# Spreading the weighted bias of a routed expert FFN over every fourth expert step

## The chip, the core and the metric

The kernel runs on one core of one Trainium2 chip. The metric is the device time of one execution in microseconds (us); lower is better. TensorE (PE), VectorE (DVE), ScalarE (ACT) and GpSimd (POOL) each work through their own queue of instructions in order; SyncE (SP) issues most transfers, and POOL issues the gathers, the scatters and the accumulating transfers. TensorE's clock has two levels, 1.2 and 2.4 GHz, and the profile gives the granted clock as a share of the upper one.

## The reference: what is computed

One layer of an encoder over 1024 tokens of 1024 channels, float32. A mixing sub-layer (Fourier branch and attention) comes first, and then the part that matters here, a routed expert FFN: each token picks 4 of 32 experts.

```python
h = xb @ w_gate_up[e] + b_gate_up[e]
gate, up = h[:, :D_EXPERT], h[:, D_EXPERT:]
gate = jnp.minimum(gate, SWIGLU_LIMIT)
up = jnp.clip(up, -SWIGLU_LIMIT, SWIGLU_LIMIT)
act = (up + 1.0) * gate * jax.nn.sigmoid(SWIGLU_ALPHA * gate)
return act @ w_down[e] + b_down[e]
...
contrib = jnp.where(buf_valid[:, None], y.astype(jnp.float32) * buf_w[:, None], 0.0)
out = jnp.zeros((n, d), jnp.float32).at[buf_tok].add(contrib)
```

After it a residual and a layer norm give the output. Since b_down does not depend on the token, the sum over a token's experts of weight times b_down is one small matrix product: (tokens x 32 weights) by (32 x 1024 biases). The kernel computes it apart from the experts.

## The kernel before

All large products are done in a split form: a float32 weight is turned into a rounded part `whi` (ACT, line 147) and a remainder `wlo` (DVE, line 148), and both are multiplied.

**Expert steps.** Each expert has 8 chunks of the gate and up product (G1, 0 to 7), for the small ones two transpositions (TR, 12 and 13), and 4 chunks of the down product (G2, 8 to 11). Every G1 or G2 chunk reads 1 MB of weights through three buffers each of `wraw`, `whi` and `wlo`. Experts are ranked by load. Those with room for more than 128 tokens form lane A, the others lane B, and `moe_plan` merges the two lanes into one list of 420 (rank, chunk) pairs, the steps. It begins: steps 0 to 3, rank 31 chunks 0 to 3 (lane B, 64 tokens); steps 4 to 6, rank 9 chunks 0 to 2 (lane A, 192 tokens); 7 and 8, rank 31 chunks 4 and 5; 9 rank 9; 10 rank 31; 11 rank 9; 12 rank 31 chunk 7; 13 to 17, rank 9 chunks 5 to 7 with rank 31's transpositions between; 18, 19, 21, 22 are rank 31's down chunks, and its result is scattered after step 22; 20, 23, 26, 29 are rank 9's down chunks; 24, 25, 27, 28, 30, 31, 33, 35 are rank 30's G1 chunks (lane B); 32, 34, 36, 38, 40 are the first G1 chunks of rank 0 (lane A, 416 tokens), and step 37 and 39 are rank 30's transpositions.

**Lane B, `rows`.** Two chunks fill one PSUM tile `psr`, of which there is one. After the second of them (an odd chunk) ACT copies half of it into an SBUF tile `gur` (line 1177), DVE adds the other half (line 1178), and the activation follows in place. `psr` is free for the next two chunks after line 1178. There are two buffers of `gur`.

**The weighted bias, `bias_out(i)`**, for 128 tokens at a time, twice 512 channels. It takes one of two PSUM tiles `psd` (lane A's down product uses the same two) and one of the same two `gur` buffers, and it adds into the accumulator `acc_d` in DRAM by an accumulating transfer on POOL's queue:

```python
ab = pep.tile([P, 512], F32, name="psd")
pe_.matmul(ab, ct[:, i, :], bd[:, ns], start=True, stop=True)
t = pe.tile([P, 2, 256], F32, name="gur").rearrange("p a f -> p (a f)")
tail[0] = act.activation(t, ab, AF.Copy)
pool.dma_start(acc_d[i * P:(i + 1) * P, ns], t, accum_op=ALU.add)
```

**Scatters.** After an expert's last down chunk its rows are added into `acc_d` by an indirect accumulating transfer on POOL's queue (line 991). Gathers of the tokens of the next expert (line 987) go through the same queue; a gather needs the expert's table of slots, which SP loads (line 1072) when the expert before is at its chunk 1.

**`overflow()`** works out on DVE, from the counts of tokens, which blocks a loop after the experts must still do. It holds one `psd` tile from its first product to line 1291, and SP writes its two small results to DRAM (lines 1297 and 1298) in the queue that loads the weights.

**Order.** The list of steps is the order in which the instructions are written, but not exactly that in which an engine gets them: a list scheduler places each engine's instructions by its own model of time, and one that is ready can be placed ahead of earlier ones. A tool inserts the semaphores. The bias is written at steps 2 to 9, `overflow()` at step 12.

Of the kernel before, what the change touches and what calls it, by code (L numbers as in the profile page):

```python
# [26 lines left out]
NX = S // P  # L27
# [79 lines left out]
def layer_kernel(ctx, tc, x, c, w_ada, b_ada, w_in, q_norm_g, k_norm_g, w_fourier, w_attn_o, w_out,  # L107
# [922 lines left out]
    with tc.tile_pool(name="pew", bufs=3, side=RIGHT) as pew, tc.tile_pool(name="pes", bufs=1, side=RIGHT) as pes, \  # L1030
# [220 lines left out]
        def bias_out(i):  # L1251

            for n in range(2):
                ns = slice(n * 512, (n + 1) * 512)
# [5 lines that stand above are left out]
# [56 lines left out]
                    e.xt(b, h, ("ptr", "psr")[h])  # L1316
        for step, (r, i) in enumerate(plan):
            e, nx = ex_[r], follow.get(r)
            if step == 12:
                with tc.issue_after(tail[0].ins):  # L1320
                    overflow()
            if 2 <= step < 2 + NX:
                bias_out(step - 2)
            if i == 0:
                e.start()
            nb_ = len(nx.blocks) if nx else 0
            if i in G1:
                if i == 1 and nx:
                    nx.table()
                e.chunk(i)  # L1330
                if 2 <= i < nb_ + 2:
                    nx.fetch(i - 2)
            elif i in TR:
                e.at(i - TR[0])
            else:
                halves = [(b, h) for b in range(nb_) for h in range(2)][2 * (i - 8):2 * (i - 8) + 2]
                e.chunk(i, [partial(nx.xt, *bh) for bh in halves])
# [143 lines left out]
```

## Time and profile before

| | us |
|---|---|
| median of 3 runs (2807.48 to 2818.73) | 2810.29 |
| the profiled execution, its own time | 2809.73 |
| its span in the profile | 2808.0 |
| PE busy in the span (91%) | 2544.5 |
| DVE busy (74%) | 2083.0 |
| ACT busy (51%) | 1421.8 |

The experts take the span from about 1047 us to about 2760 us. In the rows below a wait is put down to the instruction that ended it; matmuls are pipelined, so the time of one of them overlaps with that of the next.

### The profile page before, as it was taken

Reading aid. Unit: us, or ns where it says so; the run is one execution under the profiler, and the core shown is the slowest. Engines: PE = TensorE matmul, PEld = TensorE weight load, DVE = VectorE, ACT = ScalarE, POOL = GpSimd, SP = SyncE. Lnnn points to the kernel's source line nnn. Section 1 sums busy time; section 2 is a strip of 40 time slices with the busy share of each in tenths; the row PEclk is TensorE's granted clock in tenths of the full one; section 3 lists DMA queues with packets and bytes.
Section 4 is the critical chain, followed back from the end, with each engine's and each line's share of the span. In section 5 each row is a group of like instructions: output and inputs, shape, how many; then the busy total and the mean of one; then the engine's idle time right before and its main releaser. Section 6 shows DMA issues by size and latency. Waiting matters only on the chain. (4 is left out here: it accounts for less than half of the span.)

```text
span 2808.0 us, 43022 instructions
## 1 busy us (share of the span) xinstructions
PE 2544.5 (91%) x15948; PEld 2307.1 (82%) x15948; DVE 2083.0 (74%) x3672; ACT 1421.8 (51%) x2190; POOL 380.1 (14%) x283
## 2 busy tenths in 40 slices
PE   6999999899999947889989989989999999998991
PEld 5888899799888946789889888977888888897881
DVE  7543438777755956868788888969896888887885
ACT  3411122466621535645566556647665665665562
POOL 3100012211032232000201010011101010020003
PEclk9999999999999958999999999999999999999996
DMA  6154411000054349857889799978988898988774
GB/s 229 55 185 158 160 55 31 16 1 1 1 179 145 121 150 259 250 173 251 255 273 290 239 292 282 301 230 276 287 282 247 273 295 272 290 285 257 248 250 152
DMA packets 468742, 561.23 MB, mean 200 GB/s; under 512 B 26632, under 2 KB 404944, under 8 KB 468480
## 3 DMA queue, kind: packets, MB, share of 16 engines
q1 hardware_dynamic: 448672, 494.41, 53.9%
q0 software_dynamic: 18768, 59.64, 8.4%
q10 hardware_dynamic: 1088, 4.39, 0.5%
q8 instruction: 127, 2.08, 0.3%
q14 instruction: 87, 0.71, 0.1%
HBM read 512.90 MB, written 46.82 MB: 199 GB/s over the span
## 5 line engine op out<-in xcount | busy, mean ns | idle before, releaser
L148 DVE TENSOR_TENSOR wlo<-wraw,whi 128x1024 fp32r<-128x1024 f32 x768 | 909.7, 1217 | 220.1 <-ACT whi L147 216.0
L147 ACT ACTIVATE whi<-wraw 128x1024 fp32r<-128x1024 f32 x768 | 767.9, 1051 | 462.8 <-DMA wraw<-in_w_gate_up_dram 130.7
L1128 PE MATMUL psg<-xTa,wlo 128*128 128x160 f32 (+7 forms) x1792 | 469.5, 278 | 3.1 <-DVE wlo L148 3.0
L1128 PEld LDWEIGHTS psg<-xTa,wlo 128*128 128x128 f32 x1792 | 341.6, 194 | 8.4 <-DVE wlo L148 6.1
L1124 PE MATMUL psg<-xTa,whi 128*128 128x320 f32 (+3 forms) x1024 | 307.1, 367 | 12.4 <-ACT whi L147 10.7
L141 PE MATMUL psd<-whi,aTa 128*128 128x256 f32 (+2 forms) x768 | 220.6, 291 | 27.1 <-ACT aTa L1152 17.6
L1126 PE MATMUL psg<-xTa,whi 128*128 128x256 f32 (+3 forms) x768 | 233.3, 308 | 11.3 <-ACT whi L147 9.1
L1127 PE MATMUL psg<-xTa,whi 128*128 128x256 f32 (+3 forms) x768 | 231.9, 305 | 0.0
L143 PE MATMUL psd<-whi,aTa 128*128 128x256 f32 (+2 forms) x768 | 216.8, 287 | 3.5 <-DVE aTa L1153 3.3
L142 PE MATMUL psd<-wlo,aTa 128*128 128x256 f32 (+2 forms) x768 | 217.5, 285 | 0.1
L1124 PEld LDWEIGHTS psg<-xTa,whi 128*128 128x128 f32 x1024 | 195.8, 194 | 23.5 <-ACT whi L147 13.2
L141 PEld LDWEIGHTS psd<-whi,aTa 128*128 128x128 f32 (+2 forms) x768 | 145.7, 190 | 36.1 <-ACT aTa L1152 21.2
L1126 PEld LDWEIGHTS psg<-xTa,whi 128*128 128x128 f32 x768 | 147.4, 192 | 14.9 <-ACT whi L147 10.8
L991 POOL DMA_INDIRECT acc_d<-xya,tab x33 | 60.6, 1836 | 654.0 <-DVE xya L1215 544.2
L143 PEld LDWEIGHTS psd<-whi,aTa 128*128 128x128 f32 (+2 forms) x768 | 145.0, 190 | 5.0 <-DVE aTa L1153 4.4
L1127 PEld LDWEIGHTS psg<-xTa,whi 128*128 128x128 f32 x768 | 147.5, 192 | 1.3
L1169 PE MATMUL psr<-wlo,xTb 128*128 128x512 f32 x352 | 145.1, 412 | 3.2 <-DVE wlo L148 3.1
L142 PEld LDWEIGHTS psd<-wlo,aTa 128*128 128x128 f32 (+2 forms) x768 | 145.9, 190 | 1.3 <-DVE wlo L148 0.4
L1168 PE MATMUL psr<-whi,xTb 128*128 128x512 f32 x352 | 144.6, 411 | 2.4 <-ACT whi L147 2.4
L147 ACT ACTIVATE wh<-wraw 128x1024 fp32r<-128x1024 f32 (+1 forms) x35 | 48.1, 1377 | 154.4 <-PE psg L206 92.9
L152 ACT ACTIVATE pth<-pst 128x512 fp32r<-128x512 f32 x128 | 75.1, 599 | 86.4 <-PE pst L632 85.1
L141 PE MATMUL pz<-wh,uh 128*128 128x256 f32 x384 | 110.4, 288 | 2.4 <-DVE mrow L480 2.4
(455 smaller groups left out, 6407.5 us busy)
## 6 DMA issues: line engine op xcount, KB each, us to landing
wraw<-in_w_gate_up_dram SPq DMA_DIRECT2D x512, 512.0 KB
wraw<-in_w_down_dram SPq DMA_DIRECT2D x128, 1024.0 KB
wa<-in_w_ada_dram SPq DMA_DIRECT2D x24, 1024.0 KB
wraw<-in_w_in_dram SPq DMA_DIRECT2D x13, 1024.0 KB
xs<-in_x_dram SPq DMA_DIRECT2D x8, 512.0 KB
m_d<-sgm POOLq DMA_DIRECT2D x8, 512.0 KB, 4.1
sa_d<-sgm POOLq DMA_DIRECT2D x8, 512.0 KB, 2.9
wraw<-in_w_attn_o_dram SPq DMA_DIRECT2D x8, 512.0 KB
```

Of the source, the lines that this page charges most:

```text
L141: pe_.matmul(o, lh, rh, start=start, stop=False)
L142: pe_.matmul(o, lh, rl, start=False, stop=False)
L143: pe_.matmul(o, ll, rh, start=False, stop=stop)
L147: act.activation(hi, raw, AF.Copy)
L148: (lo_eng or vec).tensor_tensor(lo, raw, f32(hi), op=ALU.subtract)
L152: act.activation(hi, ps, AF.Copy)
L1124: pe_.matmul(ps[:, :2 * n], wh[:, k, cs], xT[:, 4 * h + k, :, :], start=first, stop=False)
L1126: pe_.matmul(ps[:, :n], wh[:, k, cs], xh, start=first, stop=False)
L1127: pe_.matmul(ps[:, :n], wh[:, k, cs], xl, start=False, stop=False)
L1128: pe_.matmul(ps[:, :n], wl[:, k, cs], xh, start=False, stop=last)
L1168: pe_.matmul(o, xk, wh[:, k, :], start=False, stop=False)
L1169: pe_.matmul(o, xk, wl[:, k, :], start=False, stop=last)
```

## The change

Two constants of the loop over the steps. `bias_out(0)` to `bias_out(7)` are written ahead of steps 8, 12, 16, 20, 24, 28, 32 and 36 in place of steps 2 to 9, and `overflow()` ahead of step 40 in place of step 12. No operation is added or removed.

```diff
         for step, (r, i) in enumerate(plan):
             e, nx = ex_[r], follow.get(r)
-            if step == 12:
+            if step == 40:
                 with tc.issue_after(tail[0].ins):
                     overflow()
-            if 2 <= step < 2 + NX:
-                bias_out(step - 2)
+            if 8 <= step < 8 + 4 * NX and step % 4 == 0:
+                bias_out(step // 4 - 2)
             if i == 0:
                 e.start()
```

## Rows read from the trace of the kernel before

**Rows 1.** Stretches: us, busy us (instructions) of PE, PEld, DVE, ACT, POOL; PEclk, DMA share, GB/s
```profile
1047.00:1135.00 88.00, 68.98 (x349) 59.89 (x349) 54.30 (x99) 51.73 (x87) 20.08 (x20) 0.86 0.82 229
1135.00:1207.00 72.00, 55.57 (x298) 47.59 (x298) 62.47 (x121) 46.02 (x66) 9.46 (x6) 0.88 0.90 280
...
1207.00:1250.00 43.00, 42.44 (x221) 41.47 (x222) 23.60 (x39) 14.37 (x26) 0.00 (x0) 0.96 0.38 127
```

**Rows 2.** Waits of PE, 1054 to 1135 us: us in total, times, longest
```profile
PE psd L1256 <- ACT gur L1258: 8.0, 3, 4.6
PE psr L1164 <- DVE gur L1178: 3.7, 1, 3.7
PE psg L1124 <- ACT whi L147: 2.6, 3, 1.0
```

**Rows 3.** Waits of PE, 1135 to 1208 us
```profile
PE psr L1164 <- DVE gur L1178: 7.5, 2, 4.7
...
PE psd L1203 <- DVE xya L1215: 1.8, 1, 1.8
PE psd L141 <- ACT aTa L1152: 1.7, 1, 1.7
PE psr L1203 <- DVE gur L1178: 1.5, 1, 1.5
```

**Rows 4.** Waits of ACT, 1054 to 1135 us
```profile
ACT gur L1258 <- DMA acc_d<-gur: 15.1, 9, 4.5
ACT gur L1177 <- DMA acc_d<-gur: 4.6, 2, 2.5
```

**Rows 5.** ACT in order of time: start, us, operation, idle before and releaser
```profile
1055.14 0.59 ACT L1177 ACTIVATE gur<-psr 64x512 f32<-64x512 f32 x1
1055.76 0.60 ACT L1258 ACTIVATE gur<-psd 128x512 f32<-128x512 f32 x1
...
1077.66 0.60 ACT L1258 ACTIVATE gur<-psd 128x512 f32<-128x512 f32 x1 [4.53 <-DMA acc_d<-gur]
...
1080.77 0.59 ACT L1177 ACTIVATE gur<-psr 64x512 f32<-64x512 f32 x1
...
1085.36 0.60 ACT L1258 ACTIVATE gur<-psd 128x512 f32<-128x512 f32 x1 [1.40 <-DMA acc_d<-gur]
...
1118.42 0.60 ACT L1258 ACTIVATE gur<-psd 128x512 f32<-128x512 f32 x1 [2.50 <-DMA acc_d<-gur]
...
1122.44 0.59 ACT L1177 ACTIVATE gur<-psr 64x512 f32<-64x512 f32 x1 [2.45 <-DMA acc_d<-gur]
...
1133.78 0.59 ACT L1177 ACTIVATE gur<-psr 64x512 f32<-64x512 f32 x1 [2.18 <-DMA acc_d<-gur]
...
1169.76 0.59 ACT L1177 ACTIVATE gur<-psr 64x512 f32<-64x512 f32 x1
```

**Rows 6.** POOL in order of time
```profile
1131.90 0.86 POOL L1259 DMA_DIRECT2D acc_d<-gur  x1 [3.41 <-ACT gur L1258]
1165.52 1.05 POOL L987 DMA_INDIRECT xyb<-u_d,tab  x1 [32.75 <-PE psr L1169]
1166.87 1.49 POOL L991 DMA_INDIRECT acc_d<-xyb,tab  x1 [0.31 <-issue]
...
1356.89 1.56 POOL L991 DMA_INDIRECT acc_d<-xya,tab  x1 [6.26 <-DMA acc_d<-xya,tab]
```

**Rows 7.** Transfers, 1054 to 1250 us: a queue's packets, MB, share; an issue's count, size, landing
```profile
q0 software_dynamic: 3616, 8.91, 20.2%
...
acc_d<-gur POOLq DMA_DIRECT2D x16, 256.0 KB, 7.3
```

**Rows 8.** SP in order of time
```profile
1155.80 0.42 SPq L1072 DMA_DIRECT2D tab<-slot_d  x1
```

**Rows 9.** PE in order of time
```profile
1028.70 1.22 PE L1256 MATMUL psd<-bd,ct 128*128 128x512 f32 x2 [0.69 <-ACT ct L929]
```

## The prediction

> **What bounds the kernel now.** I read the stretches first, to see where TensorE is not the bound. From 1207 us, when the first large expert begins, it is busy 42.44 of 43 us, and the transfer engines work at a share of 0.38. Ahead of that lie the steps that the change touches: 1047 to 1135 us (rank 31's G1 and rank 9's G1), where PE is busy 68.98 of 88 us at a granted clock of 0.86, and 1135 to 1207 us (the down chunks of both, and rank 30's G1), 55.57 of 72 us at 0.88 [rows 1]. So 19 and 16 us of PE are idle there, and some of the busy time runs at the lower of the two clock levels. No later stretch is changed by the diff.
>
> Next, what ends those waits. In the first stretch the largest is 8.0 us in which PE has the next product of the bias to do and both `psd` tiles are still waiting for ACT's copy into `gur`; then 3.7 us for `psr`, and 2.6 us for a rounded weight [rows 2]. The cause is one engine on: ACT stands 15.1 us in nine places at the copy of line 1258 and 4.6 us in two at line 1177, each time until an accumulating transfer out of `gur` has landed [rows 4]. Everything else of ACT, the rounding of weights too, is queued behind it.
>
> The order of ACT's instructions then shows who holds whom. `gur` goes round in the order in which its users are written. Between lane B's copies at 1080.77 and 1122.44 us stand ten copies of the bias, the first at 1085.36 and the last at 1118.42 [rows 5]; in the code these ten are `bias_out(2)` to `(6)`, written between chunks 3 and 5 of rank 31. One buffer is taken for 0.86 us of issue and 7.3 us to landing [rows 6, 7], so two buffers pass one copy per 4.1 us, and ten need 41 us: lane B's copies are 41.7 us apart. The bias, not the experts, paces this stretch, and lane B's weights occupy their buffers meanwhile.
>
> **The change, part by part.**
>
> *The early crowd goes.* Ahead of rank 31's chunk 5 now stand two copies instead of ten, and ahead of chunk 7 two as before; six (steps 16, 20, 24) come before rank 30's first copy. Of the waits this takes: 8.0 for `psd`, 3.7 for `psr`, and the 1.5 that rank 31's down product waits after the copy of 1133.78 us [rows 2, 3, 5], together 13.2. Pairs still go through two buffers, and six copies between the copies of steps 12 and 25 want 25 us, so I take 11; the ends are 8 (only the product's own wait) and 13.2. The late rounding, 2.6 [rows 2], goes in part: 1.5, ends 0 and 2.6. Clock: 68.98 us of work at 0.86 would take 9.7 us less at the full level [rows 1]; part of that comes from the idle time ahead of the first step and stays, so I take 4, ends 0 and 9.7. Together 16.5 us, ends 8 and 25.5.
>
> A cap on it: the transfer engines are busy 0.82 of 88 us and 0.90 of 72 us, 137 of 160 us [rows 1]; 23 us at most can be squeezed out before they are the bound. The bias' own traffic is 16 x 256 KB, 4.2 of the 8.91 MB on POOL's queue, and by bytes 18.6 of the 39.6 us (20.2% of 196) that this queue takes of all 16 engines [rows 7]. Only the pairs of steps 32 and 36, a quarter or 4.7 us, leave for the stretch with a share of 0.38. So the cap is above what I take, but not far.
>
> *`overflow()` goes to step 40.* It holds one of two `psd` tiles while rank 9's first down chunk needs them: 1.8 us of PE waiting for line 1215. Its short operations stand on DVE where DVE is busy 62.47 of 72 us; 1.7 us of PE wait there for a split that DVE and ACT deliver late [rows 1, 3]. I take 2.5, ends 0 and 3.5. At step 40 what hides it is rank 0's G1, where DVE is busy 23.60 of 43 us and no down chunk wants `psd`. Without that cover the same 3.5 us would come back. Its two small writes on SP move along; weights queued behind them are covered by the slow chunks of rank 0.
>
> *A new wait at step 24.* This is the price. Before, all bias transfers were issued by 1131.90 us and the first scatter came at 1166.87 [rows 6]; none had to wait for a scatter. Now the pair of step 24 is written behind rank 31's scatter (after step 22). Both add into `acc_d`, and where one scatter follows another the second waits: 6.26 us behind the end of the first [rows 6]. The scatter itself stood behind the gather of 1165.52 us, which needs the table that SP issued at 1155.80 [rows 6, 8]. With those times: scatter issued until 1168.36, landed 1174.6, the first transfer of the pair issued until 1175.5, landed 1182.8. Its `gur` buffer is what rank 30's first copy needs, which ran at 1169.76 [rows 5]. So that copy comes 13.0 us later, and behind it on ACT stand the rounded weights and on PE the next `psr` chunks, whose wait there is already the longest, 4.7 us [rows 3]. One down chunk of rank 9 can be done meanwhile, no more, since the next one wants `psd` behind the bias of step 28. I take 9 of the 13; the ends are 0 (the pair gets ahead, or the gather and scatter come earlier with the shorter stretch) and 13.
>
> What the Trainium skill would make of this wait: DMA: Bandwidth & Descriptors, section Anatomy of one DMA, gives a transfer on POOL's path about 2.0 us plus its bytes over 436 GB/s, so 2.6 us for 256 KB. By it, as an estimate, the buffer would be back at 1174.4 and the copy only 4.7 us late, about one chunk's cover, and the sum below would be 2792. The measured 7.3 us [rows 7] speaks against it.
>
> *The pairs of steps 28, 32 and 36.* Step 28's is followed at once by rank 30's copy of chunk 3, up to 8.2 us later; rank 9's last down chunk lies between: I take 1, ends 0 and 4. Step 32's pair waits for rank 9's two scatters, but the next lane B copy is at step 35, behind two long chunks of rank 0; step 36's has none for twelve steps. Both 0, and up to 13 each if that cover fails. PE's product for the bias is the same sixteen matmuls; two of them ran at 1028.70 in idle time [rows 9] and may do so again: 0.
>
> **Sum.** 2809.73 - 11 - 1.5 - 4 - 2.5 + 9 + 1 = 2800.7, say **2801 us**. The profiled execution lies 0.6 us under the median of the runs, 2810.29, so no correction.
>
> **Rivals.**
>
> *The new wait does not bite* (either the pair is issued ahead of the scatter, or ACT and PE have other work in hand): 2809.73 - 16.5 - 2.5 = 2791. For it: the scheduler places what is ready early, as the bias at 1028.70 shows [rows 9]. Against: `gur` and `acc_d` kept the written order in every row that I read [rows 5, 6].
>
> *Nothing comes of it*, 2810: the stretch is then bound by transfers, and what PE no longer waits for the bias it waits for weights, or the new wait takes all back. For it: a share of 0.90 in the second stretch [rows 1], and that the weights have only three buffers, so that a gap in their loading isn't made up. Against: PE's waits name `gur`, not weights from DRAM. The Trainium skill, Trainium Kernel Development and Optimization, section Key Constraints, speaks for this rival: transfers issued from SP, ACT and POOL run on the same 16 engines and interleave, so a transfer moved within a full stretch frees nothing. By that rule alone the time stays 2810; the trace agrees only so far as that three quarters of the bias' bytes stay in the two stretches with shares of 0.82 and 0.90.
>
> *Slower.* The bias pairs behind scatters each hold both `gur` buffers, and three of them (24, 28, 32) stall lane B by 13 us with no cover: 39 us against the 19 gained, 2830. It takes two and a half such waits to pass 0.5%. For it: scatters in a row wait for each other, and rank 9 has two [rows 6]. Against: only the pair of step 24 is written right behind a scatter and right ahead of a copy.
>
> **Chances.** My forecast 0.50 (its own range 2793 to 2808), no new wait 0.26, nothing 0.14, slower 0.10. A measurement of this kernel can tell about 0.5%, 14 us, from no change: faster is below 2796, slower above 2824. Of my own case about a tenth of all lies below 2796, of the case without the wait nearly all: faster 0.34, slower 0.10, same 0.56. The range leaves out the outer part of the best case (23 us, the cap, would be 2784) and of the slow one: 2786 to 2820.
>
> **What would show it.** Right: ACT's waits at lines 1258 and 1177 for landed transfers are gone ahead of step 16; lane B's second and third copies are some 15 us apart, not 42; rank 0's G1 begins near 1198 instead of 1207; PE waits 10 to 15 us for `psr` in one place at rank 30's chunk 2, while POOL's bias transfer waits for rank 31's scatter. Wrong: rank 0 begins as before although the copies are spread (transfers bind), or no bias transfer waits for a scatter, or the later part of the span, from rank 0's start to the end, differs by more than a few us, which would mean that the placing of later instructions changed with it.

## The result, and the profile after

The median goes from 2808.89 to 2780.09 us (ratio 0.9896, 95% interval 0.9872 to 0.992): faster by 29 us, 1.0%. The forecast was 2801 us, with 2786 at the low end of its range. The profiled execution of the changed kernel took 2774.33 us (span 2772.6), the fastest of its four runs; another set of runs gave it a median of 2787.18 us against 2811.33 (0.9916, 0.988 to 0.9951).

Where the time went is read with marks that both kernels have: the first product of lane B at line 1164, which opens the experts, the issue of rank 0's first scatter (the fifth of 51), the 42nd scatter and the last. The three stretches between them, of the kernel before (columns as in [rows 1], the profiled run first and a second profile of the same kernel under it):

```profile
1047.42:1349.06 301.64, 265.26 (x1487) 241.51 (x1488) 219.03 (x374) 166.58 (x252) 31.95 (x28) 0.93 0.73 224
1349.06:2490.84 1141.78, 1074.43 (x6886) 983.69 (x6885) 961.56 (x1530) 700.99 (x1019) 116.33 (x73) 0.97 0.87 276
2490.84:2759.67 268.83, 241.09 (x1546) 218.87 (x1544) 210.91 (x386) 153.82 (x263) 26.91 (x12) 0.96 0.77 241
```

```profile
1048.49:1349.99 301.50, 264.78 (x1487) 240.86 (x1488) 218.84 (x374) 166.77 (x252) 32.80 (x28) 0.92 0.73 224
1349.99:2492.53 1142.54, 1078.17 (x6890) 986.06 (x6889) 962.00 (x1530) 701.25 (x1018) 121.31 (x73) 0.97 0.87 276
2492.53:2763.49 270.96, 242.37 (x1543) 220.15 (x1541) 210.79 (x386) 154.00 (x263) 26.19 (x13) 0.95 0.76 238
```

The same stretches of the changed kernel, and of a second profile of it:

```profile
1044.79:1320.97 276.18, 254.75 (x1487) 233.09 (x1488) 219.00 (x374) 165.98 (x252) 34.45 (x28) 0.96 0.81 245
1320.97:2462.67 1141.70, 1076.50 (x6883) 983.57 (x6882) 961.71 (x1530) 700.81 (x1018) 113.02 (x74) 0.97 0.87 276
2462.67:2724.04 261.37, 236.27 (x1550) 214.83 (x1548) 210.53 (x386) 154.55 (x263) 23.40 (x13) 0.97 0.79 248
```

```profile
1047.04:1323.76 276.72, 253.68 (x1487) 231.41 (x1488) 218.82 (x374) 165.85 (x252) 32.25 (x29) 0.97 0.81 245
1323.76:2476.50 1152.74, 1081.75 (x6898) 990.23 (x6897) 961.72 (x1530) 700.74 (x1019) 121.39 (x74) 0.97 0.87 273
2476.50:2737.52 261.02, 236.41 (x1534) 215.26 (x1533) 210.90 (x386) 155.06 (x263) 27.33 (x12) 0.97 0.79 247
```

The first stretch, in which the diff lies, falls from 301.6 and 301.5 to 276.2 and 276.7 us: 25.1 by the means, and the two profiles of each kernel agree within 0.6 us. PE's 1487 instructions are the same in all four; idle time (length less busy) falls from 36.4 to 21.4, and busy time by 10.5, with the granted clock up from 0.93 to 0.96. The last stretch falls from 268.8 and 271.0 to 261.4 and 261.0, 8.7 us, although the diff touches nothing there. The middle shows no gain and varies by 11 us between the two profiles of the changed kernel; that is most of the 13 us between those two executions (2774.33 and 2787.44).

ACT's copies into `gur` in the changed kernel, where [rows 5] stood before:

```profile
1061.99 0.58 ACT L1177 ACTIVATE gur<-psr 64x512 f32<-64x512 f32 x1
1062.59 0.60 ACT L1258 ACTIVATE gur<-psd 128x512 f32<-128x512 f32 x1
...
1076.65 0.59 ACT L1177 ACTIVATE gur<-psr 64x512 f32<-64x512 f32 x1
...
1093.17 0.59 ACT L1177 ACTIVATE gur<-psr 64x512 f32<-64x512 f32 x1 [0.33 <-PE psr L1169]
...
1158.10 0.59 ACT L1177 ACTIVATE gur<-psr 64x512 f32<-64x512 f32 x1 [5.01 <-DMA acc_d<-gur]
```

Lane B's second and third copies are 14.7 us apart, not 41.7, and no copy ahead of step 16 waits for a transfer. PE's waits in the first stretch, which answer to [rows 2, 3]:

```profile
PE psd L141 <- ACT aTa L1152: 5.4, 1, 5.4
...
PE psd L1256 <- ACT gur L1258: 2.4, 1, 2.4
...
PE psr L1164 <- DVE gur L1178: 1.4, 2, 0.7
```

The bias' wait for `psd` fell from 8.0 to 2.4, lane B's for `psr` (3.7 and 7.5 before) to 1.4. The forecast's 10 to 15 us of waiting for `psr` in one place are nowhere. Rank 0's first product came at 1176.27 us in place of 1207.56, where the forecast had looked for 1198.

### The profile page after: what moved, and what is told of

It reads as the page before. It is cut to its first block, busy times and chain, and to the rows that moved or that the text cites. A ratio compares the mean times of both kernels' runs of the same rounds, so it can differ in the third digit from the quotient of the medians.

```text
span 2772.6 us, 43017 instructions
## 1 busy us (share of the span) xinstructions
PE 2529.9 (91%) x15948; PEld 2293.4 (83%) x15948; DVE 2081.1 (75%) x3672; ACT 1421.4 (51%) x2190; POOL 375.5 (14%) x283
```

## The experiments

In what follows "the stretch" is the first of the three and "the late part" the last. Medians stand beside those of the kernel before on the same chip; the lengths are from each run's profile, as the differences of the marks' start times.

| kernel | median, before | ratio (95%) | stretch | late part |
|---|---|---|---|---|
| before, two profiles | | | 301.6, 301.5 | 268.8, 271.0 |
| changed, two profiles | 2780.09, 2808.89 | 0.9896 (0.9872 to 0.992) | 276.2, 276.7 | 261.4, 261.0 |
| e1 bias only | 2783.77, 2807.96 | 0.9899 (0.9879 to 0.9919) | 275.7 | 262.9 |
| e2 search only | 2799.09, 2807.96 | 0.9963 (0.9947 to 0.9978) | 299.1 | 270.7 |
| e3 crowd at 36 to 43 | 2795.69, 2807.96 | 0.9955 (0.9934 to 0.9977) | 286.9 | 265.3 |
| e4 no bias | 2778.01, 2807.96 | 0.9885 (0.9866 to 0.9903) | 264.7 | 257.8 |
| e6 pairs at 32 to 46 | 2799.61, 2812.23 | 0.9953 (0.9935 to 0.9971) | 285.2 | 271.0 |
| e7 pairs at 2 to 16 | 2805.2, 2812.23 | 0.9976 (0.9956 to 0.9995) | 300.3 | 262.2 |
| e8 none at 24, 28 | 2787.34, 2812.23 | 0.9905 (0.9881 to 0.9929) | 276.8 | 267.6 |
| e9 pair at 23 | 2799.24, 2812.23 | 0.9942 (0.9923 to 0.9961) | 281.9 | 272.2 |
| e10 search at 20 | 2803.31, 2811.33 | 0.998 (0.9962 to 0.9997) | 298.0 | 262.6 |
| e11 changed, search at 42 | 2792.2, 2811.33 | 0.9934 (0.9909 to 0.9959) | 278.1 | 271.8 |
| e12 single copies | 2787.71, 2811.98 | 0.9909 (0.988 to 0.9938) | 281.1 | 262.5 |
| e13 single, search at 40 | 2787.67, 2811.98 | 0.9905 (0.9879 to 0.9931) | 276.2 | 274.7 |
| e14 copies on DVE | 2811.95, 2811.98 | 0.9998 (0.998 to 1.0017) | 308.0 | 268.8 |

**Which half of the diff.** e1 is the diff without its first hunk, e2 that hunk alone.

```diff
 e1
-            if 2 <= step < 2 + NX:
-                bias_out(step - 2)
+            if 8 <= step < 8 + 4 * NX and step % 4 == 0:
+                bias_out(step // 4 - 2)
 e2
-            if step == 12:
+            if step == 40:
```

> Only the bias is spread (steps 8 to 36); the search for the loop's blocks stays at step 12. Theory A, the bias copies crowd lane B out of the two gur buffers: nearly all of the gain stays, 2780 to 2787 us, ratio 0.990 to 0.993. Rival B, the search was what cost (it holds a psd tile and fills VectorE where VectorE is full): 2795 us or more. The forecast's 2.5 us for the search would give about 2783.

> Only the search moves to step 40; the bias stays at steps 2 to 9. Theory A: 2803 to 2809 us, the 0 to 3.5 us that were put on the search. Rival B: 2795 us or less.

e1 has the whole gain of the stretch, 275.7 us, and its median is in theory A's range. e2 takes 2.5 us from it, the size that the forecast gave to the search, but on top of the spread bias it brings nothing there (275.7 against 276.2 and 276.7). Its median fell by 9 us, more than the 0 to 3.5 expected, to a value between the two ranges; its late part is as long as that of the kernel before, and no stage of its one profile accounts for the rest. Rival B is out: the search alone is not what cost.

**Is it the crowd, or the place of the crowd?** e3 keeps one pair at each step but moves them to where lane B has no copy; e6 spaces them out there; e7 spaces them by two steps at the old place.

```diff
 e3 (search at 48)
+            if 36 <= step < 36 + NX:
+                bias_out(step - 36)
 e6 (search at 50)
+            if 32 <= step < 32 + 2 * NX and step % 2 == 0:
+                bias_out(step // 2 - 16)
 e7 (search at 40)
+            if 2 <= step < 2 + 2 * NX and step % 2 == 0:
+                bias_out(step // 2 - 1)
```

> The bias stays crowded, one pair at every step, but at steps 36 to 43, where lane B has no copy into gur until step 48 and lane A no down chunk; the search at step 48. Theory A (what counts is how many bias copies stand ahead of a lane B copy in the written order): as fast as the changed kernel or a few us faster, 2772 to 2784. Rival C (a crowd costs by itself, by the rate of its transfers and of ScalarE): 2795 to 2810. In the trace, theory A wants no wait of ScalarE for a landed transfer ahead of rank 0's first product.

> All eight pairs at every second step from 32 to 46, in rank 0's long chunks (one pair per 10 us or so), the search at step 50. Theory A with spacing (two things cost: copies written ahead of a lane B copy, and pairs closer together than their transfers land, which stops ScalarE's queue): neither is there, so from the first expert product to rank 0's first scatter 266 to 276 us, against 276 in the changed kernel, 287 with the crowd at step 36 and 265 without the bias; 2772 to 2783 us in all. Rival C (any place in rank 0's chunks costs, because TensorE is the bound there): 283 us or more in the stretch, 2788 or more.

> The pairs at every second step from 2 to 16, the search at step 40. Six copies instead of ten stand ahead of lane B's third copy, two in the changed kernel. Theory A: that copy comes about 6 x 4.1 us behind the second, 45 us after the first expert product (before 75, changed 32), and the stretch lies between, 284 to 292 us, 2786 to 2796 in all. Rival E (only the move of any kind matters, since it makes the scheduler order the stretch anew): as the changed kernel, 275 to 279 and 2778 to 2783.

Theory A missed both times. By the medians and e6's stretch, both runs came out in the ranges of the rivals called C: 2795.69 us for e3, 285.2 and 2799.61 us for e6. Yet a crowd that costs by itself is not the whole either: in e3 lane B is as free as in the changed kernel (its third and fourth copies come 32.0 and 51.6 us after the first product; changed 31.9 and 48.4, before 75.0 and 86.4), and 15 of the 25 us of the stretch remain. ACT's waits in rank 0's chunks, 1195 to 1260 us of e3:

```profile
ACT gur L1258 <- DMA acc_d<-gur: 17.4, 9, 4.5
```

This is [rows 4] again, 15.1 in nine places, at another place: a crowd stops ACT here too. e6 has pairs about 11 us apart on the average, and still loses 9 us against the changed kernel; a lane B copy there waited 7.7 us for a landed transfer, and transfers of the bias waited 7.5 and 4.3 us for scatters. In both runs PE waits for `psr` inside rank 0's chunks, where the changed kernel has next to no idle time. That wait, from 159 us after the first product to the end of the stretch, in e3, in e6 and in the changed kernel:

```profile
PE psr L1164 <- DVE gur L1178: 5.7, 2, 4.9
```

```profile
PE psr L1164 <- DVE gur L1178: 5.4, 2, 2.9
```

```profile
PE psr L1164 <- DVE gur L1178: 0.7, 1, 0.7
```

Only e6's first, 2.5 us, follows the copy that waited for the bias. The longest of each follows DVE's addition, which ran 5 and 4 us after ACT's copy had begun, behind rounding and operations of the search, which these runs had moved there too (steps 48 and 50). PE is also busy longer, 260.7 us in e3 and 261.0 in e6 against 254.8, with the stretch's clock at 0.94 against 0.96. So these two runs don't separate place, spacing and search. In the medians the late part adds to it: e6's, 271.0 us, has the order of the kernel before (see below). e7 fell furthest from what was expected: its stretch, 300.3, has gained nothing. Lane B's third copy came at 54.8 us, not 45, and PE stood at the product of the bias longer than before, 14.1 us against 8.0. Pairs two steps apart still met buffers that were taken: ACT stood 14.2 us in five places until a transfer had landed (1040 to 1140 us of e7):

```profile
PE psd L1256 <- ACT gur L1258: 14.1, 6, 3.9
```

So the gain is not in proportion to the copies ahead of lane B, and freeing lane B's third copy by 20 us was worth nothing by itself. The full gain came only in runs that begin at step 8 and write two copies per four steps there (changed, e1 and e11, and in other forms e8 and e13). That it needs both the distance and steps that leave PE other work is argued from these runs, not shown by one. Rival E is out as well: e7 moves the bias and has none of the stretch's gain.

**How much is left to gain.** e4 leaves the bias out; the search stands at step 40, no longer tied to the last copy of the bias.

```diff
 e4 (against the kernel before)
-            if 2 <= step < 2 + NX:
-                bias_out(step - 2)
```

> The weighted bias is left out altogether (no product, no copy, no transfer; the output lacks it); the search at step 40. Theory A: a floor little under the changed kernel, by its sixteen products (7 us of matmul time, less where PE waits anyway) and what waits are left: 2766 to 2778. Rival D (the transfers of the bias take engine time in a stretch that transfers bind): the 18.6 us that they take by bytes come off as well, 2755 to 2764.

The median is 2778.01 us, against 2780.09 and 2787.18 in the two sets of the changed kernel. The stretch is 264.7 us: of the 37 us between the kernel before and this one the change takes 25, and the bias still costs 11.5 there. Of these, 6.6 are busy time of PE, the bias' products included. Rival D, 2755 to 2764, is out by the median, and its 18.6 us are not there; that the transfers cost a smaller part of the 11.5 is not excluded.

**The wait that was forecast at step 24.** e8 takes the pairs of steps 24 and 28 away to 32 and 36; e9 writes the pair one step earlier, behind the scatter but ahead of rank 9's second down chunk.

```diff
 e8
+            for j in {8: [0], 12: [1], 16: [2], 20: [3], 32: [4, 5], 36: [6, 7]}.get(step, []):
+                bias_out(j)
 e9
+            if step in (8, 12, 16, 20, 23, 28, 32, 36):
+                bias_out((8, 12, 16, 20, 23, 28, 32, 36).index(step))
```

> As the changed kernel, but the pairs of steps 24 and 28 go to steps 32 and 36, two pairs at each. It takes away what is left of the wait that was forecast for rank 30's first copies (5.0 and 2.5 us of ScalarE in the changed kernel). If those waits still cost: stretch 270 to 274 us, 2773 to 2778. If TensorE had other work there, as its own waits say: 274 to 279, 2777 to 2784.

> As the changed kernel, but the pair of step 24 is written at step 23, ahead of rank 9's second down chunk and right behind rank 31's scatter. If the forecast's mechanism is right and only the place kept it from showing: the pair's transfer waits 4 to 8 us for the scatter's landing, rank 30's first copy comes later than 113 us after the first expert product, and the stretch grows by 4 to 10 us to 280 to 286, 2783 to 2791 in all. If the wait has no effect on TensorE wherever it stands: 274 to 279, 2777 to 2784.

Without a pair ahead of it, rank 30's first copy comes 101.4 us after the first product; in the changed kernel it comes at 113.3. So with the pair it comes 11.9 us later (the forecast had 13.0), and the stretch is the same all the same, 276.8. e8 alone doesn't prove that the delay is free, since its four pairs at steps 32 and 36 may cost what the two missing ones save; PE's own rows in the next section show it. e8's median, 2787.34 us, is above both of its ranges, and its late part, 267.6, is 6 us longer than that of the changed kernel. The reason of the delay was another one than forecast. POOL in the changed kernel:

```profile
1137.24 1.05 POOL L987 DMA_INDIRECT xyb<-u_d,tab  x1 [15.92 <-DMA tab<-slot_d]
1138.59 1.49 POOL L991 DMA_INDIRECT acc_d<-xyb,tab  x1 [0.30 <-issue]
1151.91 0.96 POOL L1259 DMA_DIRECT2D acc_d<-gur  x1 [11.83 <-ACT gur L1258]
```

The pair's transfer waits for ACT's copy at 1151.02 us, not for the scatter, which was issued 13 us before. The pair's first product ran only at 1146.41, behind rank 9's second down chunk as written, and ACT reached its copy 4.6 us later. In e9 product and copy are early (the copy ends at 1147.93), and the forecast's wait is there, POOL and then PE:

```profile
1143.58 1.49 POOL L991 DMA_INDIRECT acc_d<-xyb,tab  x1 [0.30 <-issue]
1149.53 0.96 POOL L1259 DMA_DIRECT2D acc_d<-gur  x1 [4.46 <-DMA acc_d<-xyb,tab]
```

```profile
1158.79 0.50 PE L1164 MATMUL psr<-b,sel 128*128 128x512 f32 x1 [3.53 <-DVE gur L1178]
```

POOL stood 4.46 us, of which 1.6 came after ACT's copy. PE then waited 3.53 us for rank 30's second pair, a wait that the changed kernel doesn't have, and the stretch grows to 281.9, by 5.5 from the mean of the changed kernel's two. So the forecast's chain exists and reaches PE one step away from where the edit put the pair, though the scatter is only part of it. Two expectations missed: rank 30's first copy came at 111.0 us, not later than 113, and the median, 2799.24, is above its range, with a late part of 272.2.

**The late part.** A list scheduler places the instructions by a model of time, and an edit among the first steps can shift what it places far behind. In the traces, some 590 of PE's 1550 products in the late part stand at another place of the order in the changed kernel than before; two profiles of one kernel differ in 4 and 15, which lie at the ends. e10 and e11 were chosen by the orders that the scheduler gave.

```diff
 e10 (bias as before)
+            if step == 20:
 e11 (bias as changed)
+            if step == 42:
```

> The bias as before (steps 2 to 9), the search at step 20. This place was chosen by the order that the scheduler gives: the last 5564 rows of TensorE's order of instructions (of some 14350) are those of the changed kernel, not those of the kernel before. Theory F (beside the stretch of the first experts, the edit changes the scheduler's later placing, and that is worth about 7 us after the 42nd scatter): from the first expert product to rank 0's first scatter 297 to 303 us as before, from the 42nd scatter to the last 258 to 264 us as in the changed kernel (261) and not as before (269); 2799 to 2804 in all. Rival G (the late difference is variation from run to run): 266 to 272 us there, 2805 to 2811 in all.

> The bias as changed (steps 8 to 36), the search at step 42 in place of 40. Here the last 1337 rows of TensorE's order are those of the kernel before. Theory F: stretch 274 to 279 us as changed, from the 42nd scatter to the last 266 to 272 as before, 2784 to 2790 in all. Rival G: the late part as in the changed kernel within its variation, 258 to 265, 2777 to 2783 in all.

> The kernel before once more, for a second profile: how far its stages vary from run to run. If the stages are a property of the kernel: stretch 299 to 304, from the 42nd scatter to the last 266 to 272. If they vary freely: anything from 258 to 272 in the late part.

> The changed kernel once more, for a second profile, whose first lay 6 us under the median of its runs. If the stages are a property of the kernel: stretch 274 to 279, late part 259 to 264, and the 6 us are found in the part between or ahead of them. If they vary freely: late part anywhere from 258 to 272.

The late parts of e10 and e11:

```profile
2490.23:2752.87 262.64, 238.12 (x1548) 216.26 (x1547) 210.90 (x386) 154.89 (x263) 27.19 (x13) 0.97 0.79 247
```

```profile
2466.89:2738.70 271.81, 243.61 (x1565) 220.41 (x1563) 214.41 (x391) 156.20 (x266) 21.83 (x12) 0.96 0.78 243
```

The old stretch with the changed late order takes 262.6 us there, the changed stretch with the old late order 271.8, as theory F had it, and the second profiles of both kernels repeat their own figures within 2.1 us. In the traces e10's order there is that of the changed kernel but for one product, e11's that of the kernel before but for some 150. All profiles together say the same: with the changed kernel's order, or the same but for some twenty products, 257.8 to 265.3 us (e1, e3, e4, e7, e10, e12 and the two of the kernel itself), with the order before, 268.8 to 271.0 (e6 and the two of the kernel before). Which part of the order counts is open: e2 and e14, some 100 products away from the changed kernel's, took 270.7 and 268.8. Rival G is out for this stage: 8.7 us of its length belong to an order that the edit changed by chance. In whole times it shows less plainly: e10's median lies 8.0 us under that of the kernel before, e11's, 2792.2 and just over its range, 5.0 above the changed kernel's 2787.18.

**Single copies, and copies off ACT.** e12 and e13 write the sixteen copies one by one at every second step; e14 is the kernel before with the copy on DVE.

```diff
 e12 (search at 24), e13 (search at 40)
-            for n in range(2):
+            for n in halves:
...
+            if 8 <= step < 8 + 2 * 2 * NX and (step - 8) % 2 == 0:
+                bias_out((step - 8) // 4, ((step - 8) // 2 % 2,))
 e14
-                tail[0] = act.activation(t, ab, AF.Copy)
+                vec.tensor_copy(t, ab)
```

> The sixteen copies of the bias one at a time, at every second step from 8 to 38, in place of a pair at every fourth; the search at step 24, where the later order of TensorE (the last 7363 rows) is that of the changed kernel. If a pair costs because it holds both gur buffers at once: rank 30's first copy comes 101 to 106 us after the first expert product as without a pair ahead of it (changed kernel 113), the stretch is 265 to 272 us and the time 2770 to 2778. If what is left is the products, the transfers and the scatters' waits: stretch 274 to 279, 2777 to 2787. Late part 259 to 264.

> As e12_halves, but the search at step 40, where the last 1337 rows of TensorE's order are those of the kernel before. Theory F: the stretch as in e12_halves within 3 us, the late part 266 to 272 us, so 6 to 10 us slower than e12_halves. Rival G: no difference from it.

> The kernel before, but the sixteen copies of the bias run on VectorE in place of ScalarE; steps 2 to 9 and the order of the gur buffers stay. If lane B's place behind ten copies is what costs: lane B's third copy still comes some 70 to 78 us after the first expert product (before 75), the stretch is 295 to 305 us, 2800 to 2812 in all. If it is ScalarE that stands and holds up the rounding behind it: lane B's copy is as late, but the stretch falls to 278 to 290, 2782 to 2796.

e12 and e13 don't beat the changed kernel, and e12's stretch, 281.1, is above both of its ranges. Rank 30's first copy comes at 109.2 and 108.8 us, not at 101 to 106, so single copies did not free it as a missing pair does; nothing here says that the remaining 11.5 us come from a pair's holding both buffers. Their late parts, 262.5 and 274.7, follow the order again, but their medians are equal, where theory F wanted 6 to 10 us between them; e13's stretch, 5 us shorter, and its middle, 8 us shorter, make up for it. e14's stretch is 308.0, 3 us above its first range, and lane B's third copy comes at 75.8 us: ACT's queue need not be held for the crowd to cost. But DVE stood 17.4 us at the copies in its place, so this run doesn't separate the two cleanly.

## Why the prediction was wrong

The direction was right, and a gain of 9 us was forecast where 29 were measured. By its own terms, in the stretch:

- **The early crowd and the search**: 11, 1.5 and 2.5 us of idle time to go. Measured: 15.0 (36.4 to 21.4; 13.7 by the second profiles), nearly their sum, and that by luck. By single waits it fell otherwise than written: `psd` gave 5.6 of its 8.0, and of the two waits for `psr` in rank 30's chunks, 7.5 us, which I did not count as the bias' doing, nearly all went too; the wait for rank 9's activations grew from 1.7 to 5.4 us. The search's term holds alone (e2), not on top of the spread.
- **The new wait at step 24, 9 of 13 us, and 1 for step 28: the step that failed.** The copy is late by about the amount forecast (e8: 11.9), by chance, since the reason was another; and lateness is not cost. I put the whole delay against PE but for one down chunk. In the changed order lane B runs ahead of lane A, and PE has rank 9's down products and rank 0's transpositions to do between rank 30's first two pairs; it comes to the second pair at 1159.69 us without a wait, 0.3 us after DVE's addition behind the copy of 1158.10 had ended (rows below). So of the 9 and 1 us PE paid nothing for `psr` at the second pair, by a narrow margin, and 0.7 at the third. What it does lose between the first two pairs to the bias is 2.35 and 0.69 us for the bias' own copies. The sentence that the pair waits behind the scatter was wrong for this place and right one step earlier (e9).

PE of the changed kernel, between rank 30's first and second pair, and DVE's addition:

```profile
1151.67 0.80 PE L1256 MATMUL psd<-bd,ct 128*128 128x512 f32 x1 [2.35 <-ACT gur L1258]
...
1153.15 0.58 PE L141 MATMUL psd<-whi,aTa 128*128 128x256 f32 x1 [0.69 <-ACT gur L1258]
...
1159.69 0.39 PE L1164 MATMUL psr<-b,sel 128*128 128x512 f32 x1
```

```profile
1158.73 0.68 DVE L1178 TENSOR_TENSOR gur<-psr,gur 64x512 f32<-64x512 f32 x1 [5.38 <-ACT gur L1177]
```

- **Clock, 4 us**: mis-sized. PE's busy time for the same products fell by 10.5 us (11.1 by the second profiles). The term counted the first 88 us alone, of which [rows 1] allowed 9.7; the next 72 us at 0.88 allowed another 6.7. In the changed kernel the first 87 us, the next 72 and the rest run at 0.96, 0.91 and 1.00, before at 0.86, 0.88 and 0.99. The traces have 54.9 and 58.0 us of the stretch at the lower level before, 29.9 and 27.3 after. That the shorter idle spells kept the clock up is argued, not shown.
- **The cap by transfers, 23 us**: it did not bind. The transfer share of the stretch rose from 0.73 to 0.81, and ACT now waits 16.0 us for weights, but PE only 3.7 for their rounding.
- **The late part**: not in the sum at all. I named it as a sign of being wrong ("the placing of later instructions changed"); it is worth 8.7 us by the means of two profiles.

Between the two profiled runs lie 35.4 us: 15.0 of idle and 10.5 of busy time in the stretch, 7.5 in the late part, 2.6 ahead of the first product. The medians differ by 29, and by 24 in the second set: part of the 35 is the short middle of the changed kernel's first profile. The rival without the new wait, 2791, had the right mechanism (PE had other work in hand) and lacked most of the clock and the late part.

The rule of the Trainium skill on a transfer's time (DMA: Bandwidth & Descriptors, Anatomy of one DMA), by which 256 KB take 2.6 us as an estimate, would have led nearer to the result (2792), but not for its reason. In the changed kernel's trace the transfers of the bias still land after a median of 6.1 us (5.4 in the second profile):

```profile
acc_d<-gur POOLq DMA_DIRECT2D x16, 256.0 KB, 6.1
```

The Trainium skill's statement that transfers issued from SP, ACT and POOL share the same 16 engines (Trainium Kernel Development and Optimization, Key Constraints) is not contradicted by the trace, but it did not decide: the bytes stayed in the stretch, 224 GB/s over 301.6 us and 245 GB/s over 276.2, and the time went.

Left open: what the bias' 11.5 us in the changed stretch consist of beyond its products, and whether e3 and e6 lose by the place of the bias, by its crowding or by the search beside it.

## What to carry to other kernels

Where one pool of buffers serves two streams in written order, look at the order of its users in the trace: the slower stream can pace the faster, and what helped here was distance between the slow users, among steps with slack, not merely another place (e3, e6) or a little distance (e7). A delayed instruction costs only what the engine behind it can't fill: ask for the next three pieces of work of that engine before charging a wait. And where a scheduler orders the program, compare its order far behind an edit before crediting or blaming the edit: a few us there came and went with a constant.

## What was not expected of the hardware

The middle of the experts, with the same instructions in the same order, took 1141.7 us in one profile of the changed kernel and 1152.7 in another, with PE busy 1076.5 and 1081.8 and the granted clock at 0.97 in both; the stretches ahead of and behind it agreed within 0.6 us. Over all the profiles the middle took 1139.7 to 1152.7 us, and e12, with the changed kernel's order there but for a few products, 1148.0. So a few us of a total can't be placed by one profile of each kernel, while the stretch and the late part repeated within 0.6 and 2.1 us. What lengthens the middle stays open.
